# Token sums through a matrix of ones, roots through logarithm and exponential, and an order by hand between output projection and MLP

## The chip, the core and the metric

The kernel runs on one core of a Trainium2 chip. The core has five engines that each work through a queue of their own in order and wait for one another by semaphores: TensorE (PE in the profile; its weight loads are the row PEld), VectorE (DVE), ScalarE (ACT), GpSimd (POOL) and SyncE (SP), which here only starts transfers. Transfers run on 16 DMA engines. Matrix products read from the on-chip memory SBUF and write to banks of a second one, PSUM. The metric is the device time of one execution in microseconds (us); lower is better.

## The reference

One layer of a transformer-like trunk on 512 tokens of width 1024, in float32: a root-mean-square norm, one input projection for three kinds of attention heads, one output projection into the residual, then an MLP with a short convolution and a gate, then a gated per-layer input. The change touches the two later norms and what stands around the first of them.

```python
def rms_norm(x, g):
    xf = x.astype(jnp.float32)
    y = xf * lax.rsqrt(jnp.mean(xf * xf, axis=-1, keepdims=True) + EPS)
    return (y * g.astype(jnp.float32)).astype(x.dtype)
...
        h = h + jnp.concatenate([o_a, o_b, o_c], axis=-1) @ w_out[i]
        h = h + conv_gated_mlp(rms_norm(h, ln_ffn[i]), w_up[i], conv_w[i], conv_b[i], w_down[i])
        gate = jax.nn.sigmoid(rms_norm(h, ln_ple[i]) @ w_ple_gate[i])
        h = h + (p[i] @ w_ple_proj[i]) * gate
```

## The kernel before

**Layout and products.** From the output projection on, features lie on the 128 partitions and the 512 tokens along the free dimension. The residual `h` is eight tiles `hj(0)` to `hj(7)` of 128 x 512. Every float32 product is made of three (`mm3`, line 221): each operand is split into a high part (a rounded copy, made by ACT) and a low part (the difference, made by a subtraction on DVE), and high x high, high x low and low x high are added up in a PSUM bank. So each weight tile needs a load (SP), a cast (ACT, `w_hi`) and a subtraction (`w_lo`) before PE can use it. `split` (line 205) does the last two; its tiles come from rings: six raw tiles (`raw_tile`), four with buffers of their own and two that take buffers of the rings of high and low parts, and seven high and low parts each (`in_turn`, line 191). In the rings a buffer is written again when the last instruction that reads it is through. Tiles of 128 x 512 for all else come from one pool of ten (`mtmp`, `CONV`, line 898).

**The stage around the change.** The output projection adds up eight tiles of 128 features. The first six of its eight weight rows are done earlier; `last_out(j)` (line 889) multiplies the last two (6 products of 512 columns, bank `wo`) and adds the result to `hj(j)` on DVE. Its accumulators alternate between two pairs of banks, `z` and `s`. Behind it:
- `square(j)` squares `hj(j)` on ACT; POOL adds the squares up into `sums` for j from 1 to 5, DVE for 6 and 7.
- `sum_tokens` (line 910) sums over the partitions: for each block of 128 tokens, a product of `sums` as the stationary operand with one column of ones. The result `pst` has a token per partition.
- `roots` (line 917) takes mean and power -1/2 (DVE, POOL) of these 128 x 4 numbers and multiplies an identity with them into `diag`; `spread` (line 927) turns that by a product of ones with `diag` into `pb`, a PSUM bank which holds the root of each token on every partition.
- `norm(k)` (line 1020) writes `hn` = `hj(k)` x gain x root and casts it to its high part `Th`; `low(k)` makes the low part `Tl`.
- Between these stands the product of the per-layer input, which needs nothing of `h`: `ple_cols` and `ple_load` (lines 935, 948) load and split its operands, `ple_unit(j)` (line 953, eight of them with 6 products each into `pp`) copies the result (`pps`) and stores it to DRAM (`pp_d`).

PE's order is that of the program text: eight `last_out`, three `ple_unit`, `pst`, two `ple_unit`, `pb`, three `ple_unit`, then the MLP's up-projection `u`. On ACT, DVE, POOL and SP the framework's scheduler chooses the order here, from its own estimate of readiness; `tc.high_priority` moves a block forward in that choice.

**The MLP and the end.** From the first MLP tile on the kernel plans its own order. Each piece of work is a `Task` with assumed durations, and a loop (line 1688) hands out, at each step, the task that can start and is most urgent; from there on (line 1686) ACT, DVE, POOL and SP are pinned to the planner's order. The plan starts from a list of buffers already used (`old`) and of tasks already done: loads of the up-projection weights of tiles 0 and 1, and the splits of tile 0 and of two thirds of tile 1, which are issued ahead of the plan and ordered by the scheduler. MLP tiles 0 and 1 take the features one k at a time: for k = 0 to 3 tile 0, then tile 1, 6 products each time and tile (`first`, line 1453), so the second `norm` is needed 12 products after the first. After the MLP, the last norm is formed in the same way (`sums3`, `roots3`, `spread3`, `keep3`, which copies `pb` to SBUF) while PE already multiplies the unnormalised `h` with the gate weights (`gate`, line 1579, banks `pg`); the first step of each output, `y` = `pg` x root, applies the root afterwards. The gate's accumulators go round the same four banks, so the fifth waits until the first has been read.

Of the kernel before, what the change touches and what calls it, by code (L numbers as in the profile page):

```python
# [15 lines left out]
P = 128  # L16
# [62 lines left out]
def kernel(ctx: ExitStack, tc: tile.TileContext, x, xt0, xt, pt_in, small, bias_c,  # L79
# [55 lines left out]
    dve.memset(onec, 1.0)  # L135
    ident = cp.tile([P, P], F32, tag="ident", name="ident")
# [68 lines left out]
    def split(t, n, gain=None, to=None):  # L205

        hi, lo = to or [in_turn(q, NHI)[:, :n] for q in ("hi", "lo")]
        if gain is None:
            act.copy(hi, t[:, :n])
            dve.tensor_tensor(out=lo, in0=t[:, :n], in1=f32(hi), op=ALU.subtract)  # L210
# [699 lines left out]
    def sum_tokens(tag, sums):  # L910

        pst = bank(tag, "pst")
        for t in range(NT):
            pe.matmul(pst[:, t : t + 1], sums[:, t * P : (t + 1) * P], onec, start=True, stop=True, skip_group_check=True)
        return pst

    def roots(pst):

        r = rstd.rearrange("p t c -> p (t c)")
        dve.tensor_scalar(r[:, 0:4], pst[:, 0:4], 1.0 / D, EPS, ALU.mult, ALU.add)  # L920
        pool.tensor_tensor(out=r[:, 4:8], in0=r[:, 0:4], in1=nhalf[:, 0:4], op=ALU.pow)
        dg = mtmp(F32, 1, "diag")
        dve.tensor_tensor(out=dg.rearrange("p (t c) -> p t c", t=NT), in0=ident.unsqueeze(1).broadcast_to([P, NT, P]),
                          in1=r[:, 4:8].unsqueeze(2).broadcast_to([P, NT, P]), op=ALU.mult)
        return dg

    def spread(tag, dg):

        pb = bank(tag, "pb")
        pe.matmul(pb, onec.broadcast_to([P, P]), dg, start=True, stop=True)  # L930
        return pb
# [3 lines left out]
    def ple_cols():  # L935

        pin = [mtmp(F32, 1, f"pin{k}") for k in range(2)]
        for k in range(2):
            nc.sync.dma_start(out=pin[k], in_=pt_in[k])
        hl = [mp.tile([P, 7, H], F32R, tag=tag, bufs=3, name=f"pT_{tag}").rearrange("p j c -> p (j c)") for tag in ("ah", "al")]  # L940
        hl = [[t[:, k * S : (k + 1) * S] for t in hl] for k in range(2)]
        for k in range(2):
            th, tl = hl[k]
            act.copy(th, pin[k])
            dve.tensor_tensor(out=tl, in0=pin[k], in1=f32(th), op=ALU.subtract)
            pT.append((th, tl))

    def ple_load(n, k):
        t = raw_tile()
        nc.sync.dma_start(out=t[:, :S], in_=w_ple_proj[k * P : (k + 1) * P, n * S : (n + 1) * S])  # L950
        WPP[n, k] = split(t, S)

    def ple_unit(j):
# [42 lines left out]
    for n in range(2):  # L996
        for k in range(2):
            ple_load(n, k)
# [11 lines left out]
    for j in range(3):  # L1010
        ple_unit(j)
# [763 lines left out]
```

## Time and profile before

| | |
|---|---|
| time, three runs | 719.52, 721.17, 721.29 us (median 721.17) |
| the profiled execution | 721.69 us, of which the span from the first to the last instruction is 719.9 |
| mean granted TensorE clock | 0.996 |
| PE busy | 704.1 us |
| DVE busy | 540.5 us |
| ACT busy | 389.5 us |
| POOL busy | 221.1 us |

How to read the profile's lines, here and below. A line of the timeline gives the start in us from the span's start, the duration (of the whole run of equal instructions, where xN is over 1), the engine, the line of the kernel (most instructions are recorded by one helper, L105, so they are told apart by tile names), the operation and its output and inputs; in brackets the engine's idle time just before and what ended it. A line of the view by stretches gives a stretch, its length, then the busy time and number of instructions of PE, PEld, DVE, ACT and POOL, the granted clock, the share of the DMA engines and GB/s. A line of the view of waits says who waited for whom, for how long in total, how many times and how long at most. A line of the view by groups gives the count, the total and the mean of one in ns, the idle time of the engine before it and what ended it. A line of the view by tile gives the count and the least, the median and the greatest duration in ns. A line of the list of transfers gives the count, the size and the median time from issue to landing. PE's products are pipelined: one of 512 columns has a duration of 0.39, but the next starts before it ends, so the distance from start to start is what one costs.

### The profile page before, as it was taken

What the parts mean: (1) busy time and instruction counts of PE and PEld (TensorE: products, weight loads), DVE (VectorE), ACT (ScalarE), POOL (GpSimd) and SP (SyncE); (2) the same over time, 40 slices, a digit from 0 to 9 for tenths busy, and PEclk for the clock granted to TensorE, in tenths of its full rate; (3) what the DMA queues carried; (4) which work ended last, traced back from release to release, by engine and by line L of the source; (5) the groups of instructions that cost most, each with busy time, mean ns of one, the idle gap of its engine ahead of it and who ended that gap; (6) DMA issues with size and microseconds to landing.
All of it is one profiled execution on the core that took longest, in us unless ns stands there. A gap on an engine that the chain in (4) does not pass through costs nothing.

```text
span 719.9 us, 11571 instructions
## 1 busy us (share of the span) xinstructions
PE 704.1 (98%) x4044; PEld 624.0 (87%) x4044; DVE 540.5 (75%) x1107; ACT 389.5 (54%) x732; POOL 221.1 (31%) x324
## 2 busy tenths in 40 slices
PE   9989999999999999999999999999999999999997
PEld 8978989898999888778888899988988888999786
DVE  7678887987878775678687774897776777789753
ACT  6756766775766663555445443545343555546531
POOL 4676776756665420400111101111111100001410
PEclk9999999999999999999999999999999999999999
DMA  9445658827514422644676988778886762642531
GB/s 332 177 135 153 183 168 208 287 73 212 170 59 169 147 76 75 202 145 106 145 167 125 252 196 177 193 148 228 219 190 134 179 170 66 222 160 87 177 103 59
DMA packets 48471, 116.52 MB, mean 162 GB/s; under 512 B 5494, under 2 KB 7158, under 8 KB 48412
## 3 DMA queue, kind: packets, MB, share of 16 engines
q1 hardware_dynamic: 40476, 96.59, 41.5%
q0 software_dynamic: 7648, 18.88, 16.9%
q8 instruction: 32, 0.52, 0.3%
q10 hardware_dynamic: 288, 0.30, 0.1%
q14 instruction: 27, 0.22, 0.1%
HBM read 108.53 MB, written 31.47 MB: 194 GB/s over the span
## 4 chain that ended last, share of the span: by engine, by line
PE 81%; DVE 7%; DMA 4%; ACT 3%; POOL 2%; issue 2%; SPq 0%; POOLq 0%; ACTq 0%; DVEq 0%
PE u L105 31%; PE dn_X L105 9%; PE C_z L105 6%; PE pg L105 6%; PE wo L105 5%; PE dn_Y L105 4%; PE B_z L105 4%; PE dn_Z L105 2%; DMA bias_B<-fk_d 1%; PE sX L105 1%; DMA h<-in_x_dram 1%; PE pp L105 1%; PE C_s L105 1%; PE C_po L105 1%; PE B_s L105 1%
## 5 line engine op out<-in xcount | busy, mean ns | idle before, releaser
L105 ACT CAST w_hi<-w_raw 128x768 fp32r<-128x768 f32 (+1 forms) x116 | 88.3, 784 | 75.9 <-PE dn_X L105 20.5
L105 PE MATMUL u<-Th,w_lo 128*128 128x512 f32 x320 | 126.5, 395 | 0.0
L105 PE MATMUL u<-Th,w_hi 128*128 128x512 f32 x320 | 126.5, 395 | 0.0
L105 PE MATMUL u<-Tl,w_hi 128*128 128x512 f32 x320 | 126.4, 395 | 0.0
L105 DVE TENSOR_TENSOR w_lo<-w_raw,w_hi 128x768 fp32r<-128x768 f32 (+1 forms) x116 | 102.1, 898 | 24.3 <-ACT w_hi L105 23.2
L105 DVE SCALAR_TENSOR_TENSOR c<-u,cols,c 128x511 f32<-128x511 f32 x80 | 59.6, 746 | 28.2 <-ACT c L105 27.1
L105 PEld LDWEIGHTS u<-Th,w_lo 128*128 128x128 f32 x320 | 60.1, 188 | 14.6
L105 PEld LDWEIGHTS u<-Th,w_hi 128*128 128x128 f32 x320 | 60.1, 188 | 14.2
L105 PEld LDWEIGHTS u<-Tl,w_hi 128*128 128x128 f32 x320 | 60.0, 188 | 14.2
L105 ACT ACTIVATE c<-u,cols 128x512 f32<-128x512 f32 x40 | 31.1, 777 | 30.1 <-PE u L105 30.0
L105 PE MATMUL dn_X<-g_ah,w_lo 128*128 128x256 f32 x144 | 40.7, 283 | 0.0
L105 PE MATMUL dn_X<-g_al,w_hi 128*128 128x256 f32 x144 | 40.7, 282 | 0.0
L105 PE MATMUL dn_X<-g_ah,w_hi 128*128 128x256 f32 x144 | 40.5, 281 | 0.0
L105 POOL DMA_DIRECT2D dsum<-dsum x16 | 13.0, 811 | 86.4 <-DMA dsum<-dsum 61.6
L105 POOL DMA_DIRECT2D dsum<-in_w_dadd_dram x16 | 13.1, 821 | 85.2 <-DMA dsum<-in_w_dadd_dram 64.5
L105 PE MATMUL B_z<-B_h,Th 128*128 128x384 f32 x96 | 34.5, 359 | 0.8 <-DVE B_zn L105 0.6
L105 PE MATMUL C_z<-C_h,Th 128*128 128x384 f32 x96 | 34.3, 357 | 0.0
L105 PE MATMUL B_z<-B_h,Tl 128*128 128x384 f32 x96 | 32.4, 337 | 0.0
L105 PE MATMUL B_z<-B_l,Th 128*128 128x384 f32 x96 | 32.4, 337 | 0.0
L105 PE MATMUL C_z<-C_h,Tl 128*128 128x384 f32 x96 | 32.3, 337 | 0.0
L105 PE MATMUL C_z<-C_l,Th 128*128 128x384 f32 x96 | 32.3, 337 | 0.0
L105 POOL TENSOR_TENSOR sums<-sums,n_sq 128x512 f32<-128x512 f32 x5 | 6.8, 1364 | 78.7 <-ACT n_sq L105 78.6
(498 smaller groups left out, 2093.1 us busy)
## 6 DMA issues: line engine op xcount, KB each, us to landing
w_raw<-in_w_up_dram SPq DMA_DIRECT2D x44, 384.0 KB, 5.0
dsum<-in_w_dsum_dram SPq DMA_DIRECT2D x12, 768.0 KB, 7.1
w_raw<-dsum SPq DMA_DIRECT2D x24, 384.0 KB, 5.3
w_raw<-in_w_down_dram SPq DMA_DIRECT2D x18, 384.0 KB, 4.2
w_raw<-in_w_up_dram SPq DMA_DIRECT2D x20, 256.0 KB, 4.4
B_r<-in_w_in_dram SPq DMA_DIRECT2D x12, 384.0 KB, 3.7
C_r<-in_w_in_dram SPq DMA_DIRECT2D x12, 384.0 KB, 4.7
dsum<-in_w_dadd_dram POOLq DMA_DIRECT2D x12, 384.0 KB, 6.6
```

Source lines behind the costliest of these rows:

```text
L105: ins = getattr(self.eng, op)(*a, **k)
```

## The change

The sum over the partitions is now one product: ones (128 x 128) as the stationary operand, `sums` moving, 512 columns (`total`). So `pst` already holds each token's sum on every partition, and `spread`, `diag` and POOL's power are gone. `roots` works on 128 x 512: logarithm and exponential on ACT give a first value, and four operations on DVE make one Newton step. Its result stands in SBUF, in buffers of the ring `ah`/`al` for the first norm, and for the second in the half tile that held the copy of `pb`.

The order of ACT, DVE and POOL is now pinned to the program text from `last_out` on. Each `last_out(j)` is followed by one split (of the per-layer input for j = 1 to 6, of the first MLP weights for j = 7) and then by the square. The first two loads of MLP weights are issued before this loop, the next four in it. The two casts of MLP tile 1 follow among the last `ple_unit`s, with their subtractions on POOL in place of DVE. The banks of `pp` change from alternating `z` and `s` to mostly `t`. The planner's list of used buffers and done tasks is changed to match.

```diff
@@ -133,6 +133,8 @@
     dve.memset(nhalf, -0.5)
     onec = cp.tile([P, 1], F32, tag="onec", name="onec")
     dve.memset(onec, 1.0)
+    epsc = cp.tile([P, 1], F32, tag="epsc", name="epsc")
+    dve.memset(epsc, EPS)
     ident = cp.tile([P, P], F32, tag="ident", name="ident")
     make_identity(nc, ident)
     rstd = cp.tile([P, NT, 4], F32, tag="rstd", name="rstd")
@@ -202,12 +204,12 @@
     def raw_tile():
         return in_turn("raw", NRAW)
 
-    def split(t, n, gain=None, to=None):
+    def split(t, n, gain=None, to=None, eng=dve):
 
         hi, lo = to or [in_turn(q, NHI)[:, :n] for q in ("hi", "lo")]
         if gain is None:
             act.copy(hi, t[:, :n])
-            dve.tensor_tensor(out=lo, in0=t[:, :n], in1=f32(hi), op=ALU.subtract)
+            eng.tensor_tensor(out=lo, in0=t[:, :n], in1=f32(hi), op=ALU.subtract)
         else:
             act.activation(hi, t[:, :n], AF.Copy, scale=gain)
             dve.scalar_tensor_tensor(lo, t[:, :n], gain, f32(hi), ALU.mult, ALU.subtract)
@@ -907,57 +909,54 @@
         act.activation(sq, hj(j), AF.Square)
         return sq
 
-    def sum_tokens(tag, sums):
+    def total(tag, sums):
 
         pst = bank(tag, "pst")
-        for t in range(NT):
-            pe.matmul(pst[:, t : t + 1], sums[:, t * P : (t + 1) * P], onec, start=True, stop=True, skip_group_check=True)
+        pe.matmul(pst, onec.broadcast_to([P, P]), sums, start=True, stop=True)
         return pst
 
-    def roots(pst):
-
-        r = rstd.rearrange("p t c -> p (t c)")
-        dve.tensor_scalar(r[:, 0:4], pst[:, 0:4], 1.0 / D, EPS, ALU.mult, ALU.add)
-        pool.tensor_tensor(out=r[:, 4:8], in0=r[:, 0:4], in1=nhalf[:, 0:4], op=ALU.pow)
-        dg = mtmp(F32, 1, "diag")
-        dve.tensor_tensor(out=dg.rearrange("p (t c) -> p t c", t=NT), in0=ident.unsqueeze(1).broadcast_to([P, NT, P]),
-                          in1=r[:, 4:8].unsqueeze(2).broadcast_to([P, NT, P]), op=ALU.mult)
-        return dg
-
-    def spread(tag, dg):
-
-        pb = bank(tag, "pb")
-        pe.matmul(pb, onec.broadcast_to([P, P]), dg, start=True, stop=True)
-        return pb
+    def roots(pst, rb, mt, sq):
+
+        act.activation(rb, pst, AF.Ln, scale=1.0 / D, bias=epsc)
+        dve.tensor_scalar(mt, pst, 1.0 / D, EPS, ALU.mult, ALU.add)
+        act.activation(rb, rb, AF.Exp, scale=-0.5)
+        dve.tensor_tensor(out=sq, in0=rb, in1=rb, op=ALU.mult)
+        dve.scalar_tensor_tensor(sq, sq, -0.5, mt, ALU.mult, ALU.mult)
+        dve.scalar_tensor_tensor(rb, sq, 1.5, rb, ALU.add, ALU.mult)
 
     pT, WPP = [], {}
 
-    def ple_cols():
+    def ple_splits():
 
         pin = [mtmp(F32, 1, f"pin{k}") for k in range(2)]
         for k in range(2):
-            nc.sync.dma_start(out=pin[k], in_=pt_in[k])
+            sp.dma_start(out=pin[k], in_=pt_in[k])
         hl = [mp.tile([P, 7, H], F32R, tag=tag, bufs=3, name=f"pT_{tag}").rearrange("p j c -> p (j c)") for tag in ("ah", "al")]
-        hl = [[t[:, k * S : (k + 1) * S] for t in hl] for k in range(2)]
-        for k in range(2):
-            th, tl = hl[k]
-            act.copy(th, pin[k])
-            dve.tensor_tensor(out=tl, in0=pin[k], in1=f32(th), op=ALU.subtract)
-            pT.append((th, tl))
-
-    def ple_load(n, k):
-        t = raw_tile()
-        nc.sync.dma_start(out=t[:, :S], in_=w_ple_proj[k * P : (k + 1) * P, n * S : (n + 1) * S])
-        WPP[n, k] = split(t, S)
-
-    def ple_unit(j):
-        acc = bank("zszszszs"[j], f"pp_{j}")
+        pT.extend([t[:, k * S : (k + 1) * S] for t in hl] for k in range(2))
+        todo = [lambda k=k: split(pin[k], S, None, pT[k]) for k in range(2)]
+        for n in range(2):
+            for k in range(2):
+                t = raw_tile()
+                sp.dma_start(out=t[:, :S], in_=w_ple_proj[k * P : (k + 1) * P, n * S : (n + 1) * S])
+                todo.append(lambda n=n, k=k, t=t: WPP.update({(n, k): split(t, S)}))
+        return todo
+
+    PP = {}
+
+    def ple_product(j):
+        PP[j] = acc = bank("tttzsttt"[j], f"pp_{j}")
         for k in range(2):
             a, b = (w[:, j % 4 * P : (j % 4 + 1) * P] for w in WPP[j // 4, k])
             mm3(acc, a, b, *pT[k], k == 0, k == 1)
+
+    def ple_keep(j):
         pp = mtmp(F32, 1, f"pps_{j}")
-        act.copy(pp, acc)
-        nc.sync.dma_start(out=pp_d[j], in_=pp)
+        act.copy(pp, PP[j])
+        sp.dma_start(out=pp_d[j], in_=pp)
+
+    def ple_unit(j):
+        ple_product(j)
+        ple_keep(j)
 
     U = {}
 
@@ -992,46 +991,16 @@
         _, _, _, b, c, op = PRODUCTS[what]
         dve.tensor_tensor(out=hblk(b, n, c), in0=hblk(b, n, c), in1=pv(acc), op=op)
 
-    ple_cols()
-    for n in range(2):
-        for k in range(2):
-            ple_load(n, k)
-    sums = None
-    for j in range(KD):
-        with tc.high_priority(offset=200):
-            last_out(j)
-            sq = square(j)
-            if j == 1:
-                sums = mtmp(F32, 1, "sums")
-                pool.tensor_tensor(out=sums, in0=last_sq, in1=sq, op=ALU.add)
-            elif j > 1:
-                (pool if j < KD - 2 else dve).tensor_tensor(out=sums, in0=sums, in1=sq, op=ALU.add)
-            last_sq = sq
-    for j in range(3):
-        ple_unit(j)
-    with tc.high_priority(offset=200):
-        pst = sum_tokens("o", sums)
-        dg = roots(pst)
-    for j in range(3, 5):
-        ple_unit(j)
-    pb = spread("t", dg)
     HN = {}
 
     def norm(k):
 
         HN[k] = mtmp(F32, 1, f"hn{k}")
-        dve.scalar_tensor_tensor(HN[k], hj(k), col(C_FFN, k), pb, ALU.mult, ALU.mult)
+        dve.scalar_tensor_tensor(HN[k], hj(k), col(C_FFN, k), rb2, ALU.mult, ALU.mult)
         act.copy(Th[k // 4][:, k % 4, :], HN[k])
 
     def low(k):
         dve.tensor_tensor(out=Tl[k // 4][:, k % 4, :], in0=HN[k], in1=f32(Th[k // 4][:, k % 4, :]), op=ALU.subtract)
-
-    with tc.high_priority(offset=200):
-        for k in range(2):
-            norm(k)
-            low(k)
-    for j in range(5, KD):
-        ple_unit(j)
 
     SLACK, URGENT = 0.8, 3.0
 
@@ -1396,34 +1365,82 @@
             TURN[tag].append(Slot(tag))
         return TURN[tag][-1]
 
-    old("left")
+    first_w = {}
+
+    def first_loads():
+
+        old("raw", 4)
+        old("hi", 4)
+        n = len(TASKS)
+        first_w.update((f, plain_weights(f)) for f in range(2))
+        for f in (0, 0, 1, 1, 0, 1):
+            first_w[f][2]()
+        return [q for q in TASKS[n:] if q.kind == "load"]
+
+    def first_load():
+        q = loads.pop(0)
+        q.do()
+        q.end = 0.0
+
+    def first_split(f, i, eng=dve):
+        w = first_w[f][0][i]
+        w.hi, w.lo = split(w.t, w.n, eng=eng)
+        w.split.end = 0.0
+
+    act.pinned = dve.pinned = pool.pinned = True
+    sums, todo = None, ple_splits()
+    loads = first_loads()
+    for _ in range(2):
+        first_load()
+    todo += [lambda i=i: first_split(0, i) for i in range(2)]
+    for j in range(KD):
+        last_out(j)
+        if 0 < j < KD - 1:
+            todo[j - 1]()
+            if j > 2:
+                first_load()
+        elif j:
+            todo[6]()
+        sq = square(j)
+        if j == 1:
+            sums = mtmp(F32, 1, "sums")
+            pool.tensor_tensor(out=sums, in0=last_sq, in1=sq, op=ALU.add)
+        elif j > 1:
+            (pool if j < KD - 2 else dve).tensor_tensor(out=sums, in0=sums, in1=sq, op=ALU.add)
+        last_sq = sq
+    todo[7]()
+    for j in range(3):
+        ple_unit(j)
+    rb2, work = (mp.tile([P, 7, H], F32, tag=tag, bufs=3, name=f"rb2_{tag}").rearrange("p j c -> p (j c)") for tag in ("ah", "al"))
+    rb2 = rb2[:, :S]
+    roots(total("o", sums), rb2, work[:, :S], work[:, S : 2 * S])
+    ple_unit(3)
+    first_split(1, 0, pool)
+    ple_unit(4)
+    norm(0)
+    low(0)
+    first_split(1, 1, pool)
+    ple_unit(5)
+    norm(1)
+    low(1)
+    ple_unit(6)
+    ple_unit(7)
+
+    rb_slot = old("left", 2)
     old("conv", 5)
-    HS = {k: old("conv") for k in range(2)}
-    old("conv", 3)
+    HS = {0: old("conv")}
+    old("conv")
+    HS[1] = old("conv")
+    old("conv", 2)
     for tag in ("z", "s", "t", "o"):
         old(tag, COUNT[tag])
-    pb_slot = TURN["t"][-1]
-    old("raw", 4)
-    old("hi", 4)
-
-
-    first_w = {}
-    begun = len(TASKS)
-    for f in range(2):
-        first_w[f] = plain_weights(f)
-        for _ in range(3):
-            first_w[f][2]()
-    for task in TASKS[begun:]:
-        if task.kind == "load" or task in [w.split for w in first_w[0][0] + first_w[1][0][:2]]:
-            task.do()
-            task.end = 0.0
     FORM, FORM2, us = {}, [], {}
 
     def form(k):
 
         s = HS[k] = Slot("conv")
 
-        a = Task("do", [("dve", 0.8), AC(S)], lambda: norm(k), (), [s], [pb_slot])
+        a = Task("do", [("dve", 0.8), AC(S)], lambda: norm(k), (), [s], [rb_slot])
         FORM[k] = Task("do", [DV(S)], lambda: low(k), [a], (), [s])
 
     def right_sums(i):
@@ -1562,19 +1579,13 @@
             split3(1, b, c)
     for j in range(KD):
         square3(j)
-    pst_slot, pb3_slot, dg_slot = Slot("t"), Slot("t"), Slot("conv")
+    pst_slot, root_slots = Slot("t"), [Slot("conv"), Slot("conv")]
 
     def sums3():
-        v3["pst"] = sum_tokens("t", v3["sums"])
+        v3["pst"] = total("t", v3["sums"])
 
     def roots3():
-        v3["dg"] = roots(v3["pst"])
-
-    def spread3():
-        v3["pb"] = spread("t", v3["dg"])
-
-    def keep3():
-        act.copy(v3["rb"], v3["pb"])
+        roots(v3["pst"], v3["rb"], mtmp(F32, 1, "mt"), mtmp(F32, 1, "rsq"))
 
     def gate(j, c0, c1, at_k={}):
         c = slice(c0, c1)
@@ -1609,12 +1620,8 @@
         return lambda: Task("do", [DV(n), AC(n), DV(n), DV(n)], end, [p, load_, v3["keep"]], [ys], [s, pps, sum_slot])
 
     def at_sums():
-        p = pe_task(4, sums3, (), [v3["last"]], [pst_slot], [sum_slot])
-        v3["roots"] = Task("do", [DV(4), ("pool", 1.2), DV(S)], roots3, [p], [dg_slot], [pst_slot])
-
-    def at_spread():
-        p = pe_task(8, spread3, (), [v3["roots"]], [pb3_slot], [dg_slot])
-        v3["keep"] = Task("do", [AC(S)], keep3, [p], (), [pb3_slot, sum_slot])
+        p = pe_task(8, sums3, (), [v3["last"]], [pst_slot], [sum_slot])
+        v3["keep"] = Task("do", [("act", 2.0), DV(S), ("act", 2.0), DV(S), DV(S), DV(S)], roots3, [p], root_slots, [pst_slot, sum_slot])
 
     class Rest:
 
@@ -1630,7 +1637,7 @@
     ends = []
     for j in range(KD):
         for c0, c1 in ((0, H), (H, S)) if j == KD - 1 else ((0, S),):
-            ends.append(gate(j, c0, c1, {1: {4: at_sums}, 2: {1: at_spread}}.get(j, {})))
+            ends.append(gate(j, c0, c1, {1: {4: at_sums}}.get(j, {})))
         if j > 1:
             for end in ends:
                 end()
...
```

More of the change, by code (lines that the diff above doesn't have):

```diff
@@ L1642 @@
         b.deps.append(a)
-    loads = [q for q in TASKS if q.kind == "load" and q.end is None]
-    for a, b in zip(loads, loads[1:]):
+    later = [q for q in TASKS if q.kind == "load" and q.end is None]
+    for a, b in zip(later, later[1:]):
         b.after.append(a)
```

## The prediction

> **What bounds the kernel now.** I read the page's head first, then busy time by stretch, then TensorE's (PE's) own waits, and last the order of time around the two places that the change touches.
>
> ```profile
> span 719.9 us, 11571 instructions
> PE 704.1 (98%) x4044; PEld 624.0 (87%) x4044; DVE 540.5 (75%) x1107; ACT 389.5 (54%) x732; POOL 221.1 (31%) x324
> ...
> 285.00:320.00 35.00, 33.25 (x138) 25.93 (x138) 24.28 (x37) 18.07 (x31) 7.76 (x7) 0.95 0.60 193
> 320.00:450.00 130.00, 130.00 (x672) 109.92 (x671) 95.00 (x140) 61.70 (x89) 15.23 (x19) 1.00 0.70 162
> 450.00:600.00 150.00, 150.00 (x861) 131.02 (x860) 117.30 (x174) 73.95 (x109) 17.88 (x22) 1.00 0.75 178
> 600.00:665.00 65.00, 65.00 (x472) 61.52 (x471) 51.49 (x76) 33.75 (x51) 2.58 (x2) 1.00 0.43 139
> ...
> PE pst L105 <- DVE sums L105: 1.7, 1, 1.7
> ```
>
> PE sets the end. In the stretch rows its busy time comes right after the length: from 320 to 665 us it is never idle, so whatever brings the start of that stretch forward brings the end forward by as much. The seam between output projection and MLP, 285 to 320, is the one stretch here with idle time and a granted clock (third figure from the end) under 1. The seam in order of time:
>
> ```profile
> 296.73 0.39 PE L105 MATMUL pp<-pT_ah,w_hi 128*128 128x512 f32 x1
> ...
> 300.79 0.40 PE L105 MATMUL pp<-pT_ah,w_lo 128*128 128x512 f32 x1
> ...
> 302.93 1.02 PE L105 MATMUL pst<-onec,sums 128*128 128x1 f32 x8 [1.75 <-DVE sums L105]
> 303.81 0.48 PE L105 MATMUL pp<-pT_ah,w_hi 128*128 128x512 f32 x1
> ...
> 305.07 0.51 PE L105 MATMUL pp<-pT_ah,w_lo 128*128 128x512 f32 x1
> ...
> 307.94 1.36 PE L105 MATMUL pb<-diag,onec 128*128 128x512 f32 x2
> ...
> 309.37 0.39 PE L105 MATMUL pp<-pT_al,w_hi 128*128 128x512 f32 x1
> ...
> 313.34 0.39 PE L105 MATMUL u<-Th,w_hi 128*128 128x512 f32 x1
> ...
> 318.93 0.40 PE L105 MATMUL u<-Th,w_hi 128*128 128x512 f32 x1
> ```
>
> Between the last two rows lie 24 products: a pitch of 5.59/24 = 0.233. From the first `pp` to the first `u` pass 16.61 us, in which 48 `pp` products need 11.18; 5.43 are something else. PE stood still from 301.02 (300.79 and a pitch) to 302.93, 1.91; the eight one-column `pst` products took 0.88 until 303.81; and between 305.07 and 309.37 it ran slowly: seven pitches to `pb`, `pb` at its full-clock price of 0.86 (below) and one pitch more are 2.72 of the 4.30, so 1.58 were lost. These and `pb` make 5.23; 0.2 are small waits. The slow part is a clock that was halved for one window of 3.4 us, behind a window in which PE was idle for most of 1.9 us:
>
> ```profile
> 301.79:305.20 3.41, 2.27 (x14) 2.07 (x15) 1.15 (x3) 1.29 (x3) 0.97 (x1) 1.00 0.95 267
> 305.20:308.62 3.42, 3.42 (x9) 2.39 (x8) 2.43 (x3) 1.81 (x4) 0.05 (x1) 0.50 0.65 236
> 42.40:45.82 3.42, 1.81 (x11) 1.59 (x12) 1.70 (x5) 0.84 (x2) 3.04 (x5) 1.00 0.85 223
> ```
>
> The third row, 1.81 busy and no fall in the next window, shows that scattered waits of under a microsecond do not do it. [...]
>
> The idle 1.9 us has its cause on ScalarE (ACT):
>
> ```profile
> 295.63 0.83 ACT L105 CAST w_hi<-w_raw 128x768 fp32r<-128x768 f32 x1 [2.95 <-DMA w_raw<-in_w_up_dram]
> ...
> 302.10 0.68 DVE L105 TENSOR_TENSOR sums<-sums,sq 128x512 f32<-128x512 f32 x1
> ```
>
> The cast of the first MLP weights stands in ACT's queue between the squares and waited 2.95 for its load; the squares behind it, and so the last sum, came late.
>
> **The change part by part.** Taken from the order in which the new program issues on each engine; PE's order differs only in `pst` and `pb`.
>
> *Loads.* The first two `w_up` loads now go to buffers that fall free before the last output products, and are issued ahead of two `w_ple_proj` loads; the two casts stand after squares 6 and 7. The load wait of 2.95 goes; I price it through the idle time that it caused. The eight `pp_d` stores now stand ahead of the loads for MLP tiles 2 and 3 in SP's queue, so these wait for the last `pps` copy, about 0.8 behind the last `pp`. PE needs tile 2 only 96 products (22 us) after the first `u`, and the median landing is 3.9 (first row below): the `u` products hide it with over 15 us to spare. Were that cover gone, each microsecond of lateness would cost PE one.
>
> ```profile
> w_raw<-in_w_up_dram SPq DMA_DIRECT2D x9, 384.0 KB, 3.9
> ...
> 676.82 1.09 PEld L105 LDWEIGHTS pst<-onec,sums 128*128 128x128 f32 x8
> 677.86 0.48 PE L105 MATMUL pg<-Th,w_hi 128*128 128x512 f32 x1
> ...
> 681.44 1.02 PE L105 MATMUL pb<-diag,onec 128*128 128x512 f32 x2
> 681.89 0.80 PE L105 MATMUL pg<-Th,w_hi 128*128 128x512 f32 x1
> 682.53 0.40 PE L105 MATMUL pg<-Tl,w_hi 128*128 128x512 f32 x1
> ```
>
> *PE's own work.* The new `pst` has `pb`'s form (f32, ones against 512 columns): 682.53 less a pitch less 681.44 is 0.86. In the seam it replaces 0.88, and `pb` goes. If nothing else waits, the seam is 11.18 + 0.86 = 12.04 in place of 16.61: **4.57 gained**, which holds the idle 1.91 and the lost 1.58. In the tail the old `pst` took 0.81 (676.82 and a pitch, to 677.86); it becomes 0.86 and `pb`'s 0.86 goes: **0.81 gained**. Together 5.38.
>
> *The tail's root.* Two table loads, Ln and Exp on ACT, then four VectorE (DVE) operations at 0.6 apart:
>
> ```profile
> L105 ACT ACTIVATE A_y<-A_mt x2: 621/628/634, 91.5 to 163.7; 128x512 f32<-128x512 f32 x2
> ...
> 678.37 0.72 ACT L105 ACTIVATE wg_ah<-w_raw,cols 128x512 fp32r<-128x512 f32 x1 [2.44 <-DMA w_raw<-in_w_ple_gate_dram]
> ...
> 683.12 0.69 DVE L105 TENSOR_TENSOR y<-pg,sums 128x512 f32<-128x512 f32 x1 [1.76 <-ACT sums L105]
> ...
> 683.89 1.28 ACT L105 ACT_TABLE_LOAD   x1 [0.80 <-DVE y L105]
> ...
> 692.80 0.39 PE L105 MATMUL pg<-Th,wg_ah 128*128 128x512 f32 x1
> ```
>
> They stand behind the last cast ahead of them, which waits for its load and ends at 679.1. A table load is 1.28, Ln or Exp 0.63 (the first row is such an Ln), three DVE steps 0.65 each (the first of the four runs under Exp): 679.1 + 2 x 1.91 + 1.95 + 0.7 puts the end of `y_0`'s first step at 685.6, where it was 683.8. PE next needs the bank that this step reads for `pg_4` at 692 (692.80 less 0.81). So `pg_2` and `pg_3` hide it, 6 us of cover; without them it would cost the difference, 1.8. The casts queued behind Exp on ACT are for `pg_4`'s last weights and were early by more.
>
> *What the seam adds.* Here a rival resource appears, POOL (GpSimd) beside DVE:
>
> ```profile
> 283.26 0.68 DVE L105 TENSOR_TENSOR pT_al<-pin,pT_ah 128x512 fp32r<-128x512 f32 x1
> 284.21 1.44 DVE L105 TENSOR_TENSOR pT_al<-pin,pT_ah 128x512 fp32r<-128x512 f32 x1 [0.27 <-ACT pT_ah L105]
> ...
> 283.74 1.36 POOL L179 TENSOR_TENSOR wo_l<-wo_r,wo_h 128x512 fp32r<-128x512 f32 x1 [22.48 <-ACT wo_h L105]
> ...
> 162.09 2.04 POOL L179 TENSOR_TENSOR C_l<-C_r,C_h 128x768 fp32r<-128x768 f32 x1 [2.10 <-ACT C_h L105]
> ...
> L105 POOL TENSOR_TENSOR sums<-sums,sq 128x512 f32<-128x512 f32 x4 | 5.4, 1338 | 2.9 <-ACT sq L105 2.8
> L105 ACT ACTIVATE sq<-h 128x512 f32<-128x512 f32 x8 | 5.0, 630 | 2.8 <-DVE h L105 2.7
> L105 DVE SCALAR_TENSOR_TENSOR hn<-h,cols,pb 128x512 f32<-128x512 f32 x8 | 5.8, 741 | 1.6 <-PE pb L105 1.6
> ```
>
> The same DVE subtraction takes 0.68 alone and 1.44 under a POOL one: it ends 0.55 after POOL's end (285.10), so it stood still until then. [...]
>
> The change walks into it twice. First, the splits now stand one by one between the additions to `h`, against POOL's five sums. A turn is then POOL's 1.30 and some 0.42 of split, 1.72 where PE delivers an output each 6 x 0.233 = 1.40. PE starts these outputs 48 pitches ahead of 296.73, at 285.5; the second ends at 288.5, its addition to `h` and its square (0.7 and 0.63) bring the first sum to about 290.0. The fifth ends at 290.0 + 4 x 1.72 + 1.3 = 298.2; the third split (0.55), sum 6 and the last `h` (0.6 each) reach 299.9, the first MLP split (0.87) and sum 7 301.4. PE comes to `pst` at 296.73 + 18 x 0.233 = 300.9: a wait of **0.5** (none without exclusion; 1.9 at most, as now).
>
> Second, behind `pst` (ends about 302.5) Ln waits for three copies on ACT until 302.7; Ln, Exp and three DVE steps last until 306.0, when the splits of MLP tile 1, now on POOL at 2.04 each, take their first turn. `hn`, which now reads the root from SBUF and not from PSUM, follows at 308.0 and ends at 308.7, its cast at 309.3, its low part at 310.0. PE comes to `u` at 302.3 + 30 x 0.233 = 309.3 and needs that low part one product later: 0.5 to 0.6. POOL's second turn, 310.6 to 312.7, holds tile 1's low part, 0.3, and the second `hn`'s low part, 0.1; two more splits queue ahead of the third `hn`, whose low part comes at 316.4 where PE wants it at 316.0: 0.45. Sum **1.4** (none without exclusion, since the low part of `hn` 0 would come at 307.4; at most both POOL turns in full, 4.1). I take the alternating value, since the row at 284.21 shows full exclusion.
>
> The sum: 5.38 - 0.5 - 1.4 = 3.5. The profiled span 719.9 becomes 716.4; with the 1.8 around it (that run took 721.69) 718.2, and with the median 721.17, which is 0.52 under the profiled run, **717.7**.
>
> **The rivals.**
> - *No exclusion cost.* POOL's turns fall where DVE waits for ACT anyway, and PE sees none: 5.38, so 715.8. For it: ACT hands DVE each cast with gaps; against it: three DVE steps in a row in front of `hn`.
> - *The wait only moves.* Both POOL turns lie on the path (4.1) and `pst` waits 1.9 as now: 5.38 - 6.0 = -0.6, so 721.8, no change. For it: `hn` and its low parts are one chain through ACT and DVE with POOL asking throughout; against it: only two POOL operations, and PE has 30 products of cover.
> - *Slower: the clock falls at the first `u`.* From the same two turns, if they leave PE idle for about 1.9 us within one window, two windows at half clock lose 2 x 1.6 more, on top of the moved wait: 721.8 + 3.2 = 725.0. It decides once a single wait nears 1.9; my longest is 0.6, and the row at 42.40 speaks against it.
>
> **How the numbers follow.** Alternating exclusion 0.55, no cost 0.23, moved wait 0.16, clock 0.06. A measurement here tells 0.3% (2.2 us) from no change: faster means under 719.0. That is the second case and nine tenths of the first: 0.72; the third and the rest of the first 0.22; the fourth 0.06. The runs shown of the kernel before lie 1.8 apart; with half of that, 0.9, beyond either end the range runs from the unhindered sum, 715.8 - 0.9 = 714.9, to half of the way to the moved wait, 719.8 + 0.9 = 720.7.
>
> **What would show it.** Right: `pst` once per place, 512 wide, starting within 0.6 of the last `pp` before it; no window at clock 0.5 near 305; the first `u` near 309; `hn` and its low parts stretched under POOL's `w_lo`; PE unbroken from the third `hn` on; `y_0` late but PE's `pg` unbroken. Wrong: the ACT cast still waiting for a load, a wait of PE for tile 2's weights, or a wait of `pg_4`.

## The result

| | before | after | ratio, 95% interval |
|---|---|---|---|
| median, us | 721.23 | 711.73 | 0.986 (0.9826 to 0.9895) |
| runs, us | 719.52 to 724.20 | 710.49 to 711.91 | |
| span of the profiled execution, us | 719.92 | 710.14 | |

The kernel became faster by 9.5 us. The forecast was 717.7, a gain of 3.5, with a range from 714.9 to 720.7: the sign was right, and the size was far too small.

The profile after, first the head of the page, then PE's own waits (those of the two places that the change touches):

```profile
span 710.1 us, 11539 instructions
PE 694.8 (98%) x4028; PEld 621.7 (88%) x4028; DVE 546.5 (77%) x1110; ACT 394.5 (56%) x737; POOL 223.0 (31%) x324
...
PE pst L105 <- DVE sums L105: 0.6, 1, 0.6
...
PE u L105 <- DVE Tl L105: 0.5, 2, 0.2
```

The seam in order of time, on PE:

```profile
296.51 0.40 PE L105 MATMUL pp<-pT_ah,w_hi 128*128 128x512 f32 x1
...
300.48 0.40 PE L105 MATMUL pp<-pT_ah,w_lo 128*128 128x512 f32 x1
301.46 1.09 PE L105 MATMUL pst<-sums,onec 128*128 128x512 f32 x2 [0.57 <-DVE sums L105]
301.99 0.80 PE L105 MATMUL pp<-pT_ah,w_hi 128*128 128x512 f32 x1
...
309.40 0.43 PE L105 MATMUL u<-Th,w_hi 128*128 128x512 f32 x1
310.06 0.50 PE L105 MATMUL u<-Tl,w_hi 128*128 128x512 f32 x1 [0.23 <-DVE Tl L105]
...
315.61 0.40 PE L105 MATMUL u<-Th,w_hi 128*128 128x512 f32 x1
316.23 0.50 PE L105 MATMUL u<-Tl,w_hi 128*128 128x512 f32 x1 [0.23 <-DVE Tl L105]
...
659.13 0.39 PE L105 MATMUL pg<-Th,w_hi 128*128 128x512 f32 x1
...
705.14 0.28 PE L105 MATMUL pg<-Th,wg_al 128*128 128x256 f32 x1
```

The rows that answer to these at the far end of the kernel before:

```profile
668.05 0.39 PE L105 MATMUL pg<-Th,w_hi 128*128 128x512 f32 x1
...
714.93 0.28 PE L105 MATMUL pg<-Th,wg_al 128*128 128x256 f32 x1
```

The distances between such rows split the 9.78 us of span; behind the last product both kernels take 5.0:

| stretch, us | before | after | difference | forecast |
|---|---|---|---|---|
| up to the first `pp` | 296.73 | 296.51 | -0.22 | 0 |
| first `pp` to first `u` | 16.61 | 12.89 | -3.72 | -4.07 |
| first `u` to first `pg` | 354.71 | 349.73 | -4.98 | +1.4 |
| first `pg` to last product | 46.88 | 46.01 | -0.87 | -0.81 |

So the two places that the change edits behaved nearly as forecast, and the third row, the MLP, where the work is the same, became 5 us shorter. The view by stretches shows how, in 50 us of nothing but `u` products, first before, then after:

```profile
340.00:390.00 50.00, 50.00 (x216) 40.23 (x215) 37.85 (x59) 21.57 (x33) 6.47 (x8) 1.00 0.73 152
```

```profile
340.00:390.00 50.00, 50.00 (x222) 41.43 (x221) 40.02 (x64) 23.32 (x36) 6.47 (x8) 1.00 0.74 162
```

PE is busy all the time in both, at the full clock, and passes 222 products in place of 216. Start to start, a `u` product takes 0.2333 before and 0.2271 after (means over 949 and 936 distances, waits left out). For 960 products the difference is 5.9 us. The stretch became only 4.98 shorter, since PE now waits some 1.1 at its start (the distances over 0.3 us behind the first `u`, each less a pitch). A pitch that falls while PE waits for nothing was in none of the forecast's cases.

One thing in the compiled program stands beside it. The new constant `epsc` takes 32 bytes in each partition, and the rings of weight tiles behind it in memory move up by that. By the addresses in the compiled programs the `w_hi` and `w_lo` buffers lie 96 bytes past a multiple of 256 before and 128 past it after; `Th` and `Tl`, the moving operands of `u`, lie at 128 in both.

### The profile page after: what moved, and what is told of

It is laid out like the page before. It is cut to its first block, busy times and chain, and to the rows that moved or that the text cites. A ratio compares the mean times of both kernels' runs of the same rounds, so it can differ in the third digit from the quotient of the medians.

```text
span 710.1 us, 11539 instructions
## 1 busy us (share of the span) xinstructions
PE 694.8 (98%) x4028; PEld 621.7 (88%) x4028; DVE 546.5 (77%) x1110; ACT 394.5 (56%) x737; POOL 223.0 (31%) x324
## 4 chain that ended last, share of the span: by engine, by line
PE 82%; DVE 7%; ACT 4%; DMA 3%; POOL 2%; issue 2%; DVEq 0%; ACTq 0%; POOLq 0%
PE u L105 30%; PE dn_X L105 9%; PE C_z L105 6%; PE pg L105 6%; PE wo L105 5%; PE dn_Y L105 4%; PE B_z L105 4%; PE A_z L105 3%; PE dn_Z L105 2%; DMA bias_B<-fk_d 2%; PE sX L105 1%; PE C_s L105 1%; PE C_po L105 1%; PE B_s L105 1%; DVE A_e L105 1%
## 5 line engine op out<-in xcount | busy, mean ns | idle before, releaser
L105 PE MATMUL u<-Th,w_lo 128*128 128x512 f32 x320 | 124.8, 390 | 0.0
L105 PE MATMUL u<-Th,w_hi 128*128 128x512 f32 x320 | 124.6, 389 | 0.0
```

The lines of the kernel that those rows point to most:

```text
L105: ins = getattr(self.eng, op)(*a, **k)
```

## The experiments

The address theory says that the pitch hangs on where the two operands of a product lie. Its rival, the order theory, says that the other engines' new order makes PE's products faster.

**The 32 bytes alone, put in and taken out.** The first kernel is the one before with an unused column of constants; the second the one after without its own column; the third the one after with 64 bytes more.

```diff
 (before)
     dve.memset(onec, 1.0)
+    pad = cp.tile([P, 1], F32, tag="pad", name="pad")
+    dve.memset(pad, EPS)
 (after, shifted back)
-    epsc = cp.tile([P, 1], F32, tag="epsc", name="epsc")
+    epsc = nhalf[:, 7:8]
 (after, 64 more)
+    pad = cp.tile([P, 16], F32, tag="pad", name="pad")
+    dve.memset(pad, EPS)
```

> The kernel before with one unused column of constants more, which moves the rings of weight tiles (raw, high and low parts) up by 32 bytes and leaves the order of the work and nearly all other buffers as they were. Address theory (the pitch of a 512-column product hangs on where its stationary operand lies: 32 bytes short of a multiple of 128 before, on a multiple of 128 after): the u products go from a pitch of 0.2333 to 0.2267, the time falls by about 960 x 0.0063 = 6 us to some 715. Order theory (the faster products come from the changed order on the other engines and queues): pitch 0.2333 and 721.2 as before.

> The kernel after with its constant EPS in an unused column of another tile, so that the rings of weight tiles lie where they lay before (96 modulo 128 bytes). Address theory: u pitch 0.2333, the time rises from 711.7 to about 717.6. Order theory: pitch 0.2267 and 711.7 as after.

> The kernel after with the rings of weight tiles 64 bytes higher (64 modulo 128). Address theory with a rule of 64 bytes: pitch 0.2267, 711.7. Address theory with a rule of 128 bytes: pitch 0.2333, about 717.6. Order theory: 711.7.

Measured: 712.33 for the first (ratio to before 0.9901, 0.987 to 0.9931), 717.82 for the second (0.996, 0.994 to 0.998), 716.83 for the third (0.9955, 0.9937 to 0.9973). The same 50 us in each, in this order:

```profile
340.00:390.00 50.00, 50.00 (x222) 41.42 (x221) 39.10 (x63) 21.56 (x32) 6.48 (x8) 1.00 0.72 156
```

```profile
340.00:390.00 50.00, 50.00 (x216) 40.18 (x215) 39.45 (x63) 21.73 (x33) 6.48 (x8) 1.00 0.74 160
```

```profile
340.00:390.00 50.00, 50.00 (x216) 40.26 (x215) 39.46 (x63) 22.30 (x33) 6.48 (x8) 1.00 0.76 164
```

The count goes with the address and not with the order: 222 where the weights lie at 128, 216 at 96 and at 192. The order theory falls. Beside these runs the kernel before took 719.75. So an unused column gives it 7.4 us, and the whole edit with the weights at the old addresses gives 1.9 by the medians (0.4% by the ratio); its profiled span is 716.2. The old addresses are restored for the weight rings alone: the left-hand sides `g` of the down-projection, which makes the MLP's output, lie 224 bytes past a multiple of 256 where they lay at 192 before. That this matters, and why the first gained more than 6, is seen in the next experiment.

**The map.** TensorE by itself, moving and stationary operands at chosen offsets.

```diff
+    for n in (512, 256):
+        for mo in OFFS:
+            for so in OFFS:
...
+                for i in range(24):
+                    tc.keep_in_program_order(nc.tensor.matmul(acc[:, :n], ST[so][:, i % 8 * P : (i % 8 + 1) * P], MV[mo][:, i % 4 * S : i % 4 * S + n],
+                                     start=i == 0, stop=i == 23))
```

> TensorE alone: none of the layer is computed and the output holds one product's values; 24 products for each pair of a moving and a stationary offset (a, b, c, d: 0, 32, 64, 96 bytes past a multiple of 128), first with 512 columns, then with 256. Address theory, stationary operand: 512-column pitch 0.227 for stationary a (and c, if the rule is 64 bytes) and 0.233 for the others, whatever the moving operand. A rival, the moving operand: the pitch goes by the moving offset. Order theory: one pitch in all sixteen.

Neither operand alone decides, so all three readings written down beforehand failed. Here each row is 24 products; the second figure is the time of all of them, 23 pitches and the last product's 0.39:

```profile
15.82 5.76 PE L108 MATMUL b<-mva,stb 128*128 128x512 f32 x24
21.42 5.76 PE L108 MATMUL b<-mva,stc 128*128 128x512 f32 x24
...
38.23 5.63 PE L108 MATMUL b<-mvb,stb 128*128 128x512 f32 x24
43.71 5.76 PE L108 MATMUL b<-mvb,stc 128*128 128x512 f32 x24
...
54.90 5.67 PE L108 MATMUL b<-mvc,sta 128*128 128x512 f32 x24
...
66.02 5.64 PE L108 MATMUL b<-mvc,stc 128*128 128x512 f32 x24
```

In the names the letter of the moving operand (`mv`) comes first, that of the stationary one (`st`) second. Of these rows the pairs with equal offsets (b and b, c and c) are fast, c with a is half fast, and the others are slow, a with c among them: what counts seems to be the distance, moving less stationary address. The second map tests that with more offsets and another base.

```diff
+    for n, so, mos in ((512, 0, (7, *range(8))), (512, 2, range(8)), (256, 0, range(8)), (256, 2, range(8)), (384, 0, range(8))):
+        for mo in mos:
```

> TensorE alone, as in the map before, none of the layer: stationary operands at 0 (sta) and 64 (stc) bytes past a multiple of 256, moving operands at 0 to 224 in steps of 32 (mva to mvh); 24 products a pair, with 512 columns, then 256, then 384 (sta only). Distance theory (the first map read as a rule: what counts is moving less stationary address, modulo 256): at 512 columns 0.2267 at distance 0, 0.2288 at 64, 0.2333 elsewhere; at 256 columns 0.1133 at distance 192, 0.1178 at 64, 0.120 at 0 and 96; with stc the same figures two offsets on. Rival, absolute addresses: with stc the figures don't move on by two offsets.

Its timeline with the stationary operand at 64 bytes (the list goes from a moving offset of 0 to one of 160; then 256 columns at 0 and 64):

```profile
71.91 5.76 PE L106 MATMUL b<-mva,stc 128*128 128x512 f32 x24
77.50 5.75 PE L106 MATMUL b<-mvb,stc 128*128 128x512 f32 x24
83.09 5.61 PE L106 MATMUL b<-mvc,stc 128*128 128x512 f32 x24
88.54 5.77 PE L106 MATMUL b<-mvd,stc 128*128 128x512 f32 x24
94.14 5.67 PE L106 MATMUL b<-mve,stc 128*128 128x512 f32 x24
99.65 5.77 PE L106 MATMUL b<-mvf,stc 128*128 128x512 f32 x24
...
139.10 2.90 PE L106 MATMUL b<-mva,stc 128*128 128x256 f32 x24
...
144.67 3.04 PE L106 MATMUL b<-mvc,stc 128*128 128x256 f32 x24
```

The pattern moved on with the base, so the distance theory holds. From the starts in the trace, ns a product, stationary operand at 0:

| distance, bytes modulo 256 | 0 | 32 | 64 | 96 | 128 | 160 | 192 | 224 |
|---|---|---|---|---|---|---|---|---|
| 512 columns | 227.2 | 233.4 | 228.8 | 234.0 | 233.4 | 234.3 | 233.3 | 233.4 |
| 384 columns | 174.5 | 173.4 | 173.4 | 176.7 | 176.0 | 176.7 | 174.7 | 174.1 |
| 256 columns | 120.0 | 117.8 | 117.8 | 119.7 | 118.7 | 117.4 | 113.4 | 118.2 |

Set against this the kernels, whose distances follow from their addresses (means over the trace's starts, waits left out; the down-projection's products have 256 columns, and only the four fifths of them that read `g` are taken here, since the others lie at other distances in some of these kernels):

| kernel | `u`: distance, ns | down-projection from `g`: distance, ns |
|---|---|---|
| before | 32, 233.3 | 96, 119.8 |
| after | 0, 227.1 | 96, 120.0 |
| before, 32 bytes more | 0, 227.1 | 64, 117.8 |
| after, shifted back | 32, 233.3 | 128, 118.6 |
| after, 64 more | 192, 233.3 | 32, 117.3 |

For `u` each figure agrees with the map to within 0.1 ns, for the down-projection to within 0.5. The first experiment's surplus is the down-projection: 924 products x 2.0 ns are 1.8 us. And of the 1.9 us that the kernel shifted back gains on the one before, some 0.9 is this too: 756 products from `g` x 1.2 ns.

**A version that uses it.** The rings that hold the down-projection's moving operands are moved as well.

```diff
-    tok = mp.tile([P, 1], F32, tag="tok", name="tok")
...
     rb2 = rb2[:, :S]
+    tok = mp.tile([P, 1], F32, tag="tok", name="tok")
+    shift = mp.tile([P, 32], F32, tag="shift", name="shift")
```

> The kernel after with the rings of the MLP's left-hand sides (g_ah, g_al, and wg_ah, wg_al, pT_ah, pT_al, which share them) and xh, xl moved to 64 modulo 256 bytes, the weight rings staying at 128 as after; the order of all work is that of after. Distance theory: the down-projection's 256-column products read g at a distance of 192 from the weights (96 after) and go from 0.120 to 0.1133, 756 products x 6.5 ns = 4.9 us; xh, xl and the gate's products some 0.8 more: about 706. Rival (distance matters at 512 columns only, or the down-projection waits for something else): 711.7.

Measured: 709.03 (0.9842, 0.9815 to 0.9869), the fastest kernel of this study by its median; its interval overlaps that of the kernel after. The first `u` to the first `pg` took 347.00 where after took 349.73. Half of the expected gain came: the down-projection's mean pitch fell to 117.2 and not to 113.3. Most of its products took 117 to 119, and 120 of them, all between 440 and 457 us, took 113 or 114. The next run asks whether the kernel's way of using each high weight tile twice in a row is the cause.

```diff
+                mm(to, WH[:, a], GH[o][:, b], first, False)
+                mm(to, WH[:, a], GL[o][:, b], False, False)
+                mm(to, WL[:, a], GH[o][:, b], False, last)
```

> TensorE alone, none of the layer: the products in the kernel's own triples (high weights twice, with a high and a low moving part, then low weights), weights at 0 modulo 256 bytes, both moving parts at 0 to 224 in steps of 32; 36 products a distance, with 512 columns and then with 256. Open is why the down-projection took 0.117 at distance 192 and not the map's 0.1133. If the repeated weight tile decides it: at 256 columns about 0.1175 at 64 and at 192, 0.120 at 96; at 512 columns 0.2267 at 0 as in the first maps. If the triples make no difference: 0.1133 at 192 again, and the cause lies in the kernel's other traffic.

It isn't: at 192 the triples took 113.3, and all other means agree with the table to 0.5 ns. Nor is it how far apart the buffers lie beyond 256 bytes: 87 pairs of operands with the very same two addresses took 113 or 114 between 440 and 457 us and 117 to 119 at other times, one of them 118 at 414.3 and 113 at 445.5. So at this distance the addresses alone do not decide, and why most of the kernel's products take 117.7 stays open. The other engines' traffic was not tested.

**The root without the order.** The new sums and root in the kernel before, the rest left to the scheduler.

```diff
     with tc.high_priority(offset=200):
-        pst = sum_tokens("o", sums)
-        dg = roots(pst)
+        rb2, work = (mp.tile([P, 7, H], F32, tag=tag, bufs=3, name=f"rb2_{tag}").rearrange("p j c -> p (j c)") for tag in ("ah", "al"))
+        rb2 = rb2[:, :S]
+        roots(total("o", sums), rb2, work[:, :S], work[:, S : 2 * S])
     for j in range(3, 5):
         ple_unit(j)
-    pb = spread("t", dg)
```

> The kernel before with the new sums and roots in both places, but the order between output projection and MLP left to the scheduler and the loads, casts, banks and addresses as before (EPS in an unused column of another tile). If the seam's gain comes from the order by hand, as the prediction has it: PE's wait of 1.9 before pst stays, pb's 0.86 goes in both places, and the longer root (two ACT and four DVE operations) may make the first u wait; 1.7 us less at best, about 719. If the root alone brings it, as a rival: 717.8, what the whole change makes at the old addresses.

Measured: 720.26, ratio 0.9998 (0.9979 to 1.0017): nothing. Its rows on PE:

```profile
302.90 1.10 PE L105 MATMUL pst<-sums,onec 128*128 128x512 f32 x2 [1.47 <-DVE sums L105]
311.32 0.50 PE L105 MATMUL u<-Th,w_hi 128*128 128x512 f32 x1 [0.32 <-ACT Th L105]
312.80 0.50 PE L105 MATMUL u<-Tl,w_hi 128*128 128x512 f32 x1 [0.97 <-DVE Tl L105]
```

The wait before `pst` stays, and the longer root is late at the first `u`. The order by hand, with the loads, casts and banks that belong to it, takes most of both away: with it, the same root and the same weight addresses (after, shifted back) the time was 717.8, PE waited 0.53 before `pst` (1.64 here, distances less a pitch) and 0.43 for the low part behind the first `u` (1.24 here).

```profile
302.22 1.09 PE L105 MATMUL pst<-sums,onec 128*128 128x512 f32 x2 [0.36 <-DVE sums L105]
```

The order was not tried with the old root. The profiled span of the root alone did fall, to 718.4: no window ran at half clock there (1.00 in each of three stretches up to 665), and the tail was 0.89 shorter. Both come back below.

**DVE standing still under POOL.** After, DVE and POOL at the first root and the first normalised tile, one fence for each engine:

```profile
304.76 0.69 DVE L105 SCALAR_TENSOR_TENSOR rb_al<-rb_al 128x512 f32<-128x512 f32 x1
305.48 2.36 DVE L105 SCALAR_TENSOR_TENSOR rb_ah<-rb_al,rb_ah 128x512 f32<-128x512 f32 x1
307.88 0.75 DVE L105 SCALAR_TENSOR_TENSOR hn<-h,cols,rb_ah 128x512 f32<-128x512 f32 x1
```

```profile
305.45 1.84 POOL L105 TENSOR_TENSOR w_lo<-w_raw,w_hi 128x768 fp32r<-128x768 f32 x1 [7.36 <-DVE rb_al L105]
310.09 2.29 POOL L105 TENSOR_TENSOR w_lo<-w_raw,w_hi 128x768 fp32r<-128x768 f32 x1 [2.80 <-ACT w_hi L105]
```

The last step of the root takes 2.36 in place of 0.69. It ends at 307.84, 0.55 behind POOL's end at 307.29, the same 0.55 as in the forecast's row. The next kernel gives POOL's two splits to DVE.

```diff
-    first_split(1, 0, pool)
+    first_split(1, 0)
...
-    first_split(1, 1, pool)
+    first_split(1, 1)
```

> The kernel after with the two subtractions of MLP tile 1's first weights on DVE in place of POOL. If DVE and POOL shut each other out at the first u products, as the prediction has it: the normalised tiles come without POOL's turns, but each split takes 0.9 of DVE ahead of them; the waits of 0.43 and 0.39 at the first and fifth u group shrink by half or so, 711.3. If the exclusion costs nothing here: the splits lengthen DVE's chain and the time rises by up to 1 us, 712.5.

Measured: 711.94 (0.9875, 0.9852 to 0.9898), level with the kernel after. The same step of the root on DVE, then PE:

```profile
305.19 0.69 DVE L105 SCALAR_TENSOR_TENSOR rb_ah<-rb_al,rb_ah 128x512 f32<-128x512 f32 x1
```

At 0.69, and with no POOL split beside it, the step no longer stands still. The first four groups of six `u` products run through, but the fifth, which reads the third normalised tile, waits:

```profile
315.29 0.50 PE L105 MATMUL u<-Th,w_hi 128*128 128x512 f32 x1 [0.49 <-ACT Th L105]
316.01 0.50 PE L105 MATMUL u<-Tl,w_hi 128*128 128x512 f32 x1 [0.23 <-DVE Tl L105]
```

So the standstill is real (2.36 beside POOL's split, 0.69 without it), and taking it away in this manner gains PE nothing: what DVE gains, it spends on the splits, 0.95 and 0.96 here. Neither expectation's figure can be told from the other by the time.

**The wait before `pst`.** On top of the aligned rings, one split is moved behind the last sum. In this kernel two weight tiles change places in their ring, so that a later split overwrites one of them early and the output is not that of the layer; the number of instructions is the same.

```diff
-        if 0 < j < KD - 1:
+        if 0 < j < KD - 2:
             todo[j - 1]()
...
+        elif j == KD - 2:
+            first_load()
...
+    todo[5]()
     todo[7]()
```

> The kernel with the aligned rings, and one subtraction of the per-layer input's weights moved from between the additions to h to behind the last sum. If DVE's turns with POOL set pst, as the prediction has it: PE's wait of 0.75 before pst falls to 0.1 or less, the first u comes 0.7 earlier, about 708.4. If the last square on ACT sets it: no change, 709.0.

Measured: 709.33 (0.9853, 0.9829 to 0.9878), no gain over the aligned rings:

```profile
301.14 1.09 PE L105 MATMUL pst<-sums,onec 128*128 128x512 f32 x2 [0.34 <-DVE sums L105]
309.41 0.50 PE L105 MATMUL u<-Th,w_hi 128*128 128x512 f32 x1 [0.17 <-ACT Th L105]
310.14 0.50 PE L105 MATMUL u<-Tl,w_hi 128*128 128x512 f32 x1 [0.22 <-DVE Tl L105]
```

The wait before `pst` shrank from 0.76 to 0.51 (distances of the starts, less a pitch), and the first `u` now waits 0.33. On DVE one sum stood 0.77 for its square on ACT, with the last addition to `h` queued behind it. Both theories had named a part. That the chain through ACT and DVE as a whole is as long as PE's cover would explain it; it was not tested further.

## Why the prediction was wrong, point by point

- **The step that failed is the pitch.** The forecast took 0.233 for a 512-column product from the trace of before and carried it through the MLP as a constant. The diff's `epsc`, which shifts all weight buffers, stands in none of its terms. The pitch fell to 0.2271, 5.9 us over the 960 products of `u`. No rival reached the case either: the lowest, 715.8, was made of terms of the seam and the tail only. The shift alone was worth 7.4 on the old kernel and 6.1 on the new one (717.82 less 711.73, from two series of runs).
- **What was left of the forecast without the shift: partly luck.** With the weights shifted back the whole change took 717.82 and a span of 716.2, where the forecast had 717.7 and 716.4. But the forecast counted 3.5 from a median of 721.17 in three runs, and beside 717.82 the kernel before took 719.75: a gain of 1.9, of which some 0.9 is the down-projection's distance, a term that the forecast did not have.
- **The seam's gain, 4.57 less 0.5 for `pst`: right for the profiled execution.** First `pp` to first `u` took 12.89, forecast 12.54. The load wait of ACT's cast is gone, `pst` is one product of 512 columns, no window near 305 is at half clock (granted 1.00 from 301.79 to 308.62). `pst` came at 301.46, where DVE's turns with POOL had put it, 301.4; the wait was 0.74 and not 0.5, since PE now came earlier.
- **The clock's share: right in size, its condition too simple.** The half window went with the wait, as forecast. But the kernel with the root alone kept a wait of 1.64 (1.87 from start to start, less a pitch) and ran on at full clock (1.00 from 301.79 to 308.62). The half window is also not in every execution of the kernel before: one of 3.4 us takes 0.0024 off the mean granted clock, and of 35 later runs 18 had 0.999 or 1.0 (718.5 to 720.6 us), where the forecast's profiled run had 0.996. So the 1.58 is a gain over some executions only.
- **The start of `u`, 1.4: mechanism right, size somewhat too large.** Two waits came, at the low parts of the first and of the fifth group (the forecast's `hn` 0 and 2), 0.43 and 0.40 from the starts less a pitch, where 0.5 to 0.6 and 0.45 were forecast. The terms of 0.3 for tile 1's low part and 0.1 for the second `hn` came to 0.1 together. With 0.1 more at the product behind each of the two waits it is the 1.1 above.
- **The tail, 0.81: right.** With the root alone, at the old addresses, it became 0.89 shorter. In the kernel after it was 0.87: `y_0` came late behind two table loads and no wait of `pg` followed, but faster `pg` products (228.0 in place of 233.3 ns where they read `w_hi` and `w_lo`, 84 of them: 0.4), slower ones where they read `wg`, whose distance moved from 192 to 160 (0.3), and a first wait for `Tl` that is 0.2 longer are in it too.
- **The loads: right.** PE waited for no weights of tiles 2 and 3.
- **The rivals.** *No exclusion cost* and *the wait only moves* lie on either side of what the seam did; the clock did not fall at `u` (1.00 from 309 to 320).

## What to carry to other kernels

A diff that allocates anything moves what lies behind it: compare the buffer addresses of the two compiled programs, of both operands of each product, before taking a duration over from the old trace. Where PE is busy all the time, the pitch itself is a term: 2.7% of each 512-column product hung here on the distance of its two operands modulo 256 bytes, more than the whole reordering was worth. And to know what an edit brings, measure it at the old addresses.

## What the runs showed of the hardware

**The distance of PE's two operands.** In the maps, at full clock and with no other engine at work, a product of 512 columns took 226.7 to 234.5 ns, one of 256 columns 113.3 to 120.0, by the distance of moving and stationary address. The best distance differs: 0 at 512 columns, 192 at 256. Why the time hangs on it was not tested.

**The halved clock.** In the traces of the layer's kernels, ahead of their last products, the clock fell to half three times, for 3.42 us each time: in the kernel before, in that with 32 bytes more and in the aligned one. In the kernel before it fell once more behind the last product, at 718.22, 413.0 us after 305.20, some 121 times 3.41. That the clock goes by windows of this length is an estimate from these figures; the windows below are of that length. The third fall is far from any edit:

```profile
41.90:45.31 3.41, 1.61 (x11) 1.13 (x10) 1.34 (x5) 0.83 (x2) 3.27 (x4) 1.00 0.91 236
45.31:48.73 3.42, 3.42 (x15) 3.42 (x13) 2.93 (x5) 1.27 (x3) 2.59 (x6) 0.51 0.32 55
```

PE was busy for 1.61 of the window ahead of it, with scattered waits of 1.14 at most. The forecast's row at 42.40 had 1.81, waits of 1.09 at most and no fall behind it, so the forecast's reading that scattered waits do not do it was wrong. The window around `pst` in the kernel before was busy for 2.27, and in that with 32 bytes more for 1.79, of which the one-column products made 0.88 and 0.89:

```profile
301.49:304.90 3.41, 1.79 (x13) 1.66 (x13) 1.67 (x4) 1.31 (x4) 0.46 (x1) 0.99 0.80 223
304.90:308.32 3.42, 3.42 (x10) 2.65 (x9) 2.43 (x3) 2.02 (x3) 0.56 (x1) 0.51 0.64 237
```

The window of the root alone, with its wait of 1.64 and no one-column products, had 1.94 and no fall:

```profile
300.27:303.68 3.41, 1.94 (x8) 1.07 (x7) 2.48 (x4) 2.16 (x5) 0.00 (x0) 1.00 0.50 117
```

So far this would fit a limit between 1.61 and 1.81 of busy time, the one-column products left out, an estimate from these five windows. The kernel after with 64 bytes more speaks against that:

```profile
145.73:149.14 3.41, 1.54 (x10) 1.21 (x8) 1.78 (x10) 0.57 (x2) 1.97 (x3) 1.00 0.09 32
149.14:152.56 3.42, 3.30 (x22) 3.13 (x23) 3.22 (x18) 2.78 (x10) 1.85 (x4) 1.00 0.11 41
...
149.26 0.47 PE L105 MATMUL B_s<-B_k_k,B_q_q 128*128 128x512 f32 x1 [1.99 <-DVE B_st L105]
```

PE was busy for 1.54 of the first of these windows and idle for 1.86 at its end, in a single stretch that lasted 1.99 in all, and no fall followed. In the kernel before, 1.14 us of the idle stretch ahead of `pst` lay in the window that was followed by a fall. So neither PE's busy time in the window nor the length of an idle stretch decides by itself. All products of that first window have 256 or 384 columns, where the three ahead of a fall hold products of 1 or 128 columns too. But so does the one at 42.40, and what decides was not shown.
